# Output projection with two token tiles' products ahead of the last quotient instead of four; first up weights split behind the last values

## The chip, the cores and the metric

The kernel runs on one core of a Trainium2 chip. The metric is the device time of one execution in microseconds (us). The core has five engines that run side by side, each with its own instruction queue in fixed order: TensorE (PE in the profile; PEld is its weight load), VectorE (DVE), ScalarE (ACT), GpSimd (POOL) and SyncE (SP), which here issues nearly all DMAs. Engines wait for each other by semaphores. Matmul results land in PSUM, in banks of 128 x 512 float32; all else on the chip lies in SBUF. The 128 partitions are the first number of every tile shape.

## The reference, cut to what matters

One decoder block on 1024 tokens of width 1024. Eight attention heads of width 64 with a forgetting bias and a gated part of width 512 run side by side; their outputs, concatenated, go through the output projection and are added to the input. A gated MLP with a causal convolution follows, then a last norm.

```python
    mix = jnp.concatenate([att, sg], axis=-1)
    h = h + mix @ w_out[layer]
    h = h + conv_ffn(rmsnorm(h, norm_ffn_g[layer]), w_up[layer], conv_w[layer],
                     conv_b[layer], w_down[layer])
return rmsnorm(h, norm_final_g)
```

In `forgetting_attention` each row of weights is a softmax: exponentials divided by their sum. The kernel multiplies the exponentials with the values first and divides by the row sums at the end. This division is what the title calls the quotient.

## The kernel before, in words

All matmuls work in a reduced-precision form of float32 that the kernel makes up for by splitting: a tensor x becomes a high part (a cast) and a low part (x minus the high part), and a product is three matmuls: high x high, high x low, low x high. `split_w` (L160 to L166) does this for weights: the cast on ACT, the subtraction on DVE. For the up and down projections the kernel uses a seven-product scheme (Strassen, Winograd's form) with block names A11, A12, A21, A22 for weights and S1 to S4 for their sums; the sums of raw weights are made on POOL (`upw_b`, L1271 to L1283). For the first two of the 22 column blocks of the up projection these sums are written in place, over the raw weights that A11 and A12 were split from: so POOL can begin as soon as the split of A11 has read them.

**The end of attention.** Heads are handled in pairs; `attF[p]` (tag H) holds the undivided result of pair p in its first half and the broadcast reciprocals of the row sums in its second. The last values are matmuls at L1054; ACT copies one half of a result (L1062), DVE adds the other (L1063). The reciprocals travel through DRAM: ACT's queue writes them (L943), SP reads them back as a broadcast (L944). Then `pair_half` forms the quotient (L957), casts its high part into `attT[p]` (L958) and subtracts for the low part (L959), in two halves of 512 tokens: 512 to 1023 first, then 0 to 511. For pairs 0 to 2 this is POOL's work, hidden under later heads; for pair 3, the last, it is done by DVE and ACT, and nothing of attention is left to hide it.

**The output projection.** The product of the gated half has been made earlier and stored as `hpd`. What is left is `att @ w_out[:512]`: eight token tiles of 128 (index tt), two column halves (hf), four pairs (k), three matmuls each, 24 matmuls per tile (`wmm`, L1303 to L1305). The tile of `attT` is the stationary operand, the weights move. For tiles 0, 4, 1 and 5 the products of pairs 0 to 2 are made first, into eight PSUM banks, since they need no pair 3: 72 matmuls. Then, tile by tile (0, 4, 1, 5, 2, 3, 6, 7), the rest is accumulated, `hload` brings in `hpd` (L1309), `hadd` adds (DVE, L1313), `norm2` forms the norm (ACT L1320, L1321, DVE L1322, L1323) and stores `h2d` (SP, L1324), and `flip` transposes the normed tile on PE in eight transpositions (L1341) and splits it into the operands of the up projection (L1327 to L1358). Tiles tt and tt + 4 are combined there, which is why their order is interleaved.

**What sets the order.** A scheduler places instructions by its own estimates of time within the data dependencies and the extra orderings that the code adds with `after(later, earlier)`; from then on each engine keeps that order. `seq` chains PE's instructions in the order in which they are written: it was used up to the last values, not in `wmm` and `flip`. `behind` orders an instruction behind one kept in `gates`. The splits of the first up weights (raw tiles loaded at L1252, `upw_a`) went into tag `wha` of a pool that only exists once attention's buffers are released. Tag `x1` held the heads' query and key tiles, two buffers of 128 x 2 x 1024.

Of the kernel before, what the change touches and what calls it, by code (L numbers as in the profile page):

```python
# [14 lines left out]
P = 128  # L15
# [54 lines left out]
def block_kernel(ctx: ExitStack, tc: tile.TileContext, xT, xtok, wuv, wuh, wv0, wva, wvk, wvl, wqk, cpk, bfv,  # L70
# [5 lines left out]
    sml = ctx.enter_context(tc.tile_pool(name="sml", bufs=4))  # L76
    early = tc.alloc_tile_pool(name="early", bufs=1)
# [13 lines left out]
    BUFS = {"x1": 2, "x2": 2, "t3": 1, "t2": 1, "t01": 1, "V": 4, "H": 4, "wy": 2, "gg": 2,  # L91
# [4 lines left out]
    def sb(tag, shape, dt=F32):  # L96
        return (raws if tag == "raw" else late if tag in LATE else early).tile(shape, dt, tag=tag, bufs=BUFS[tag], name=nm(tag))

# [58 lines left out]
    def split_w(src, hl, hi_eng="act", lo_eng="dve"):  # L157
        h, l = hl
        if hi_eng == "act":
            act.copy(h, src)  # L160
# [5 lines left out]
        return eng.tensor_tensor(out=l, in0=src, in1=f32(h), op=ALU.subtract)  # L166

    gates = {}
# [9 lines left out]
    def xset(tags):  # L178
        return [sb(t, [P, 2, 2, 512], F32R) for t in tags]
# [5 lines left out]
    def xs(n, hl, k):  # L185
        return XS[n][k // 2][:, hl, k % 2, :]

    def x2(n, hl, j):
        return XS[n][j][:, hl, :, :]
# [433 lines left out]
    def emit(t, dst, i, parts, src=None):  # L623
        for o in parts:
# [5 lines left out]
            for j in range(2):  # L630
                floors["sp"] = sp.dma_start(out=dst[2 * i + j].rearrange("s d t -> d s t")[:, :, o], in_=t[j * 64:(j + 1) * 64, :, o])

# [80 lines left out]
    floors = {}  # L713
# [16 lines left out]
    xy = sb("x1", [P, 2, 1024])  # L730
    xl = sb("pt", [P, 1024])
    sp.dma_start(out=xl, in_=vx[0])
    after(tc, sp.dma_start(out=xy, in_=vx[1:3].rearrange("a p c -> p a c")), floors["ld"])
    for i, o in ((0, ALU.subtract), (1, ALU.add)):
        after(tc, dve.tensor_tensor(out=xy[:, i], in0=xy[:, i], in1=xl, op=o), newest[0])
    vw["S1"] = pairs(l21)

# [130 lines left out]
    def head_loads(h):  # L868
        ab = sb("x1", [P, 2, 1024], F32R)
        abs_[h] = ab  # L870
        hh = h % 2
        sp.dma_start(out=f32(ab[:, 0, :]), in_=qd[h].rearrange("s d t -> (s d) t"))
        for s in range(2):
            sp.dma_start(out=f32(ab[s * 64:s * 64 + 64, 1, :]), in_=kd[h, 0])
# [10 lines left out]
    va_, vb_, vc_ = xy[:, 0], xy[:, 1], xl  # L885
# [61 lines left out]
    def pair_half(p, o):  # L947
# [8 lines left out]
        else:  # L956
            dve.tensor_tensor(out=f[:, 0, o], in0=f[:, 0, o], in1=f[:, 1, o], op=ALU.mult)  # L957
# [18 lines left out]
    def logits_mm(h, j, ps):  # L976
        A, B, A2, B2 = abs_[h][:, 0, :], abs_[h][:, 1, :], a2s[:, h % 2, :], b2s[:, h % 2, :]
# [237 lines left out]

    for o in (slice(512, 1024), slice(0, 512)):
        pair_half(3, o)


    after(tc, act.activation(pad[:, 0:1], eps, AF.Sqrt), last_copy)  # L1220
# [20 lines left out]
    def ut_(pool_, tag, shape, dt, bufs):  # L1241
        return pool_.tile(shape, dt, tag=tag, bufs=bufs, name=nm(tag))

    xt = {n: xtp.tile([P, 4, 512], F32, tag="xt" + n, name="xt" + n) for n in ("B11", "B21", "B22")}

    AHEAD = 2
    split_of = {}

    def upw_a(i):

        wr = sb("raw", [P, 2, 512])
        d = sp.dma_start(out=wr, in_=wup[i, :, 2:4, :])  # L1252
        if i < AHEAD:
            after(tc, d, loads[7])
        out = {"ra": wr}

        def split(names):
            for n in names:
                t = ut_(upl, "wha", [P, 2, 512], F32R, 4)
                split_of[n] = split_w(wr[:, ("A11", "A12").index(n), :], (t[:, 0], t[:, 1]))  # L1260
                behind(split_of[n], "sums" if i < AHEAD else "hg")
                out[n] = t
            return out

        return out, split
# [33 lines left out]
    def wmm(tt, hf, ps, ks_):  # L1299
        ts_ = slice(tt * P, (tt + 1) * P)  # L1300
        for k in ks_:
            w = wo[k][hf]
            pe.matmul(ps, attT[k][:, 0, ts_], w[:, 0, :], start=(k == 0), stop=False)  # L1303
            pe.matmul(ps, attT[k][:, 0, ts_], w[:, 1, :], start=False, stop=False)
            pe.matmul(ps, attT[k][:, 1, ts_], w[:, 0, :], start=False, stop=(k == 3))  # L1305
# [27 lines left out]
    def flip(tt):  # L1333
# [3 lines left out]
        for kh in range(2):  # L1337
            ps = sbank()
            for j in range(4):
                k = 4 * kh + j  # L1340
                pe.transpose(ps[:, j * P:(j + 1) * P], xn[tt][:, k * P:(k + 1) * P], ident)  # L1341
# [18 lines left out]

    WA = [upw_a(i) for i in range(AHEAD)]
    W = [WA[0][1](("A11", "A12"))]
# [5 lines left out]
    W.append(WA[1][1](("A11", "A12")))  # L1368
    WB = [upw_b(0, W[0], True), upw_b(1, W[1], True)]
    prev = None  # L1370
    for tt in (0, 4, 1, 5, 2, 3, 6, 7):
        hload(tt)
        for hf in range(2):
            if tt in first:
                wmm(tt, hf, banks8[tt, hf], (3,))
                hadd(tt, hf, banks8[tt, hf])
            else:
                ps = bank()
                wmm(tt, hf, ps, range(4))
                hadd(tt, hf, ps)  # L1380
        norm2(tt)
        if prev is not None:
            flip(prev)
        prev = tt
# [236 lines left out]
    RING = {"xr": (upl, "sg", 4), "xh": (upl, "wha", 4), "wh": (upr, "whb", 6)}  # L1621
# [223 lines left out]
```

## Time and profile before

| | us |
|---|---|
| time, median of 3 runs (lowest to highest) | 1046.32 (1046.3 to 1047.15) |
| the profiled execution's own time | 1046.16 |
| its span, first to last instruction | 1044.4 |
| PE busy in the span | 1036.8 |
| DVE / ACT / POOL busy | 893.3 / 562.8 / 222.6 |
| start of the output projection on PE | 357.45 |
| first matmul there that reads the last quotient | 373.87 |

Times in the trace are counted from the first instruction. A timeline row gives start, length, engine, line, operation, output <- inputs, partitions x elements, how many, and in brackets how long the engine stood idle before and what ended that wait. Rows with a count merge instructions of one kind that follow each other; their length runs from the first's start to the last's end. An instruction on DVE or ACT can start some 0.1 us before the one ahead of it has ended, so lengths add up to a little more than the time that passes.

### The profile page before, as it was taken

What the parts mean: (1) busy time and instruction counts of PE and PEld (TensorE: products, weight loads), DVE (VectorE), ACT (ScalarE), POOL (GpSimd) and SP (SyncE); (2) the same over time, 40 slices, a digit from 0 to 9 for tenths busy, and PEclk for the clock granted to TensorE, in tenths of its full rate; (3) what the DMA queues carried; (4) which work ended last, traced back from release to release, by engine and by line L of the source; (5) the groups of instructions that cost most, each with busy time, mean ns of one, the idle gap of its engine ahead of it and who ended that gap; (6) DMA issues with size and microseconds to landing.
All of it is one profiled execution on the core that took longest, in us unless ns stands there. A gap on an engine that the chain in (4) does not pass through costs nothing.

```text
span 1044.4 us, 14270 instructions
## 1 busy us (share of the span) xinstructions
PE 1036.8 (99%) x4998; PEld 870.0 (83%) x4998; DVE 893.3 (86%) x1302; ACT 562.8 (54%) x1003; POOL 222.6 (21%) x167
## 2 busy tenths in 40 slices
PE   9999999999999999999999999999999999999997
PEld 7988888988888888788888888888888888888886
DVE  6899887988888779998999998898997866997774
ACT  6777632457776747644444444443544544454654
POOL 0000232500322540353334323323331000000000
PEclk9999999999999999999999999999999999999999
DMA  9622558885745533231354431332422998333432
GB/s 331 235 85 95 153 156 250 232 259 170 203 135 167 201 134 130 81 120 62 121 168 146 142 121 67 127 111 73 129 81 83 325 337 292 112 92 101 144 118 101
DMA packets 67452, 161.66 MB, mean 155 GB/s; under 512 B 8095, under 2 KB 9239, under 8 KB 67381
## 3 DMA queue, kind: packets, MB, share of 16 engines
q1 hardware_dynamic: 67108, 160.72, 47.9%
q8 instruction: 39, 0.64, 0.3%
q14 instruction: 33, 0.26, 0.1%
q10 hardware_dynamic: 272, 0.04, 0.0%
HBM read 115.68 MB, written 45.05 MB: 154 GB/s over the span
## 4 chain that ended last, share of the span: by engine, by line
PE 98%; DVE 1%; ACT 0%; issue 0%; ACTq 0%; DVEq 0%
PE k L1656 20%; PE qc L1396 12%; PE qa L1396 11%; PE qd L1396 11%; PE qb L1396 5%; PE pb L270 5%; PE ps L270 5%; PE pb L1054 3%; PE pb L1038 3%; PE qc L509 2%; PE qd L509 2%; PE qa L509 2%; PE pl L984 2%; PE ps L853 2%; PE pl L985 2%; PE pf L1078 1%
## 5 line engine op out<-in xcount | busy, mean ns | idle before, releaser
L1656 PE MATMUL k<-whb,wha 128*128 128x512 f32 (+1 forms) x936 | 209.9, 387 | 0.0
L1656 PEld LDWEIGHTS k<-whb,wha 128*128 128x128 f32 x936 | 174.1, 188 | 35.8 <-DVE wha L166 0.2
L1396 PE MATMUL qc<-xT,whb 128*128 128x512 f32 x540 | 129.8, 389 | 0.1
L1396 PE MATMUL qa<-xB,wha 128*128 128x512 f32 x528 | 127.5, 390 | 0.0
L1396 PEld LDWEIGHTS qc<-xT,whb 128*128 128x128 f32 x540 | 101.3, 188 | 21.5 <-ACT whb L160 0.5
L1396 PEld LDWEIGHTS qa<-xB,wha 128*128 128x128 f32 x528 | 98.8, 188 | 20.9 <-DVE wha L166 0.4
L160 ACT CAST wha<-sg 128x512 fp32r<-128x512 f32 x77 | 47.8, 622 | 96.6 <-PE k L1656 84.9
L160 ACT CAST whb<-sg 128x512 fp32r<-128x512 f32 x82 | 50.5, 618 | 87.9 <-PE qc L1396 67.6
L166 DVE TENSOR_TENSOR wha<-sg,wha 128x512 fp32r<-128x512 f32 x77 | 52.8, 688 | 39.0 <-ACT wha L160 38.9
L1396 PE MATMUL qd<-xB,whb 128*128 128x512 f32 x264 | 63.7, 389 | 0.0
L1396 PE MATMUL qd<-xT,whb 128*128 128x512 f32 x264 | 63.7, 390 | 0.0
L1396 PE MATMUL qb<-xT,whb 128*128 128x512 f32 x252 | 61.0, 390 | 0.0
L166 DVE TENSOR_TENSOR whb<-sg,whb 128x512 fp32r<-128x512 f32 x82 | 57.0, 697 | 4.4 <-ACT whb L160 4.3
L1280 POOL TENSOR_TENSOR sg<-raw 128x512 f32<-128x512 f32 x20 | 31.0, 1550 | 139.4 <-DVE whb L166 76.2
L1039 ACT CAST pt<-pb 128x512 fp32r<-128x512 f32 x72 | 40.1, 583 | 36.0 <-PE pb L1038 23.7
L1396 PEld LDWEIGHTS qd<-xT,whb 128*128 128x128 f32 x264 | 49.5, 188 | 10.5 <-DVE u L1503 0.3
L1396 PEld LDWEIGHTS qd<-xB,whb 128*128 128x128 f32 x264 | 49.6, 188 | 10.3
L1396 PEld LDWEIGHTS qb<-xT,whb 128*128 128x128 f32 x252 | 47.2, 188 | 10.0 <-DVE whb L166 0.3
L1040 DVE TENSOR_TENSOR pt<-pb,pt 128x512 fp32r<-128x512 f32 x72 | 47.3, 686 | 9.6 <-ACT pt L1039 8.9
L1054 PE MATMUL pb<-pt,V 128*128 128x512 f32 (+3 forms) x192 | 49.4, 362 | 0.4 <-DVE pt L1040 0.3
L1283 POOL TENSOR_TENSOR sg<-sg,raw 128x512 f32<-128x512 f32 x20 | 33.3, 1664 | 63.5 <-DVE whb L166 63.5
L1281 POOL TENSOR_TENSOR sg<-sg,raw 128x512 f32<-128x512 f32 x20 | 35.1, 1756 | 47.2 <-issue 44.6
(431 smaller groups left out, 2247.6 us busy)
## 6 DMA issues: line engine op xcount, KB each, us to landing
raw<-wup SPq DMA_DIRECT2D x44, 512.0 KB
sg<-hx SPq DMA_DIRECT2D x77, 256.0 KB
hx<-hs SPq DMA_DIRECT2D x44, 256.0 KB
hx<-ca SPq DMA_DIRECT2D x35, 256.0 KB
xT<-wdn SPq DMA_DIRECT2D x28, 256.0 KB
x<-kd SPq DMA_DIRECT2D x24, 256.0 KB
A<-xtok SPq DMA_DIRECT2D x8, 512.0 KB
raw<-wqk SPq DMA_DIRECT2D x8, 512.0 KB
```

Source lines behind the costliest of these rows:

```text
L160: act.copy(h, src)
L166: return eng.tensor_tensor(out=l, in0=src, in1=f32(h), op=ALU.subtract)
L270: pe.matmul(banks[m], xs(n, xi, k)[:, ms], w[:, wi, :], start=(first and k == 0 and c == 0 and (own or m % 2 == 0)), stop=(k == 3 and c == ...
L509: pe.matmul(ps, w[:, wi, ks], xs(n, xi, k), start=(first and c == 0), stop=(c == 11), skip_group_check=True)
L1038: seq(pe.transpose(ptr[:, o:o + P], places[g[0], j // 2][j % 2][:, k * P:(k + 1) * P], ident))
L1039: casts.append(act.copy(pt[:, 0, :], ptr))
L1040: los.append(dve.tensor_tensor(out=pt[:, 1, :], in0=ptr, in1=f32(pt[:, 0, :]), op=ALU.subtract))
L1054: seq(pe.matmul(po[half][:, o:o + w], lhs, pt[:, s, c:c + w], start=(new and s == 0), stop=(s == 1 and (half, k) in ((1, 6), (0, 3))), ski ...
L1281: pool.tensor_tensor(out=s[1], in0=s[0], in1=a11, op=ALU.add)
L1283: pool.tensor_tensor(out=s[3], in0=s[1], in1=a12, op=ALU.add)
L1396: pe.matmul(ps, w[:, wi, ks], xb[:, xi, k, :], start=(first and n == 0), stop=(n == 11), skip_group_check=True)
L1656: pe.matmul((banks[bk + m] if ps is None else ps)[:, o], xh[:, xi, ms], wh[:, wi, o], start=((first and p_ == 0 or new) and n == 0), stop= ...
```

## The change

Five edits, of which the first two are named in the title.

1. `AHEAD`, `upw_a` and its splits move ahead of `pair_half(3, ...)`. The four splits (A11 and A12 of the first two column blocks) are ordered behind the last copy of the values on ACT (`last_copy`), and the first multiplication of the last quotient is ordered behind the last of the four on DVE (`gates["own"]`). The table load for the square root follows the last cast.
2. Only tiles 0 and 4 are started ahead of the quotient: 36 matmuls in four banks.
3. `wmm` and `flip` (but for tile 7's) are chained with `seq`, so PE runs them as written; a table `FLIP` says behind which tile and half each tile's transpositions stand.
4. To have a home before attention's buffers are released, the splits go into tag `x1`, which becomes four buffers of half the size in a pool of its own (`base`); query and key tiles and the value sums become two tiles each. Later splits of A11 and A12 and the down projection's `xh` use the same buffers.
5. The load of the value sums is two DMAs instead of one, with orderings among stores and additions.

```diff
+            m = dve.tensor_tensor(out=f[:, 0, o], in0=f[:, 0, o], in1=f[:, 1, o], op=ALU.mult)
+            if gates:
+                after(tc, m, gates.pop("own"))
...
+            for n in names:
+                t = ut_(base, "x1", [P, 2, 512], F32R, 4)
+                split_of[n] = split_w(wr[:, ("A11", "A12").index(n), :], (t[:, 0], t[:, 1]))
+                if i < AHEAD:
+                    after(tc, cast[0], last_copy)
+                else:
+                    behind(split_of[n], "hg")
...
+    WA = [upw_a(i) for i in range(AHEAD)]
+    W = [a[1](("A11", "A12")) for a in WA]
+    gates["own"] = split_of["A12"]
     for o in (slice(512, 1024), slice(0, 512)):
         pair_half(3, o)
-    after(tc, act.activation(pad[:, 0:1], eps, AF.Sqrt), last_copy)
+    after(tc, act.activation(pad[:, 0:1], eps, AF.Sqrt), cast[0])
...
-    first = (0, 4, 1, 5)
-    banks8 = {(tt, hf): (bank() if hf == 0 else sbank()) for tt in first for hf in range(2)}
-    for hf in range(2):
-        for tt in first:
-            wmm(tt, hf, banks8[tt, hf], (0, 1, 2))
+    early_ = ((0, 0), (4, 0), (0, 1), (4, 1))
+    banks8 = {(tt, hf): (bank() if hf == 0 else sbank()) for tt, hf in early_}
+    for tt, hf in early_:
+        wmm(tt, hf, banks8[tt, hf], (0, 1, 2))
...
+    FLIP = {(1, 1): 0, (5, 0): 4, (2, 0): 1, (3, 0): 5, (6, 0): 2, (7, 0): 3, (7, 1): 6}
     for tt in (0, 4, 1, 5, 2, 3, 6, 7):
         hload(tt)
         for hf in range(2):
-            if tt in first:
-                wmm(tt, hf, banks8[tt, hf], (3,))
-                hadd(tt, hf, banks8[tt, hf])
-            else:
-                ps = bank()
-                wmm(tt, hf, ps, range(4))
-                hadd(tt, hf, ps)
-        norm2(tt)
-        if prev is not None:
-            flip(prev)
-        prev = tt
+            ps = banks8[tt, hf] if (tt, hf) in early_ else bank()
+            wmm(tt, hf, ps, (3,) if (tt, hf) in early_ else range(4))
+            hadd(tt, hf, ps)
+            if hf:
+                norm2(tt)
+            if (tt, hf) in FLIP:
+                flip(FLIP[tt, hf])
```

How the built programs differ, first on DVE at the end of attention. Before (H is `attF[3]`, G is `attT[3]`, wha the split weights, raw the raw ones, pt the loaded `hpd`, pb and ps PSUM banks):

```order
L1063 TENSOR_TENSOR H_3593<-pb_3828,H_3593 64x512
L957 TENSOR_TENSOR H_3593<-H_3593 128x512 x2
L959 TENSOR_TENSOR G_3839<-H_3593,G_3839 128x512 x2
L166 TENSOR_TENSOR wha_3872<-raw_3868,wha_3872 128x512
L166 TENSOR_TENSOR wha_3875<-raw_3868,wha_3875 128x512
L166 TENSOR_TENSOR wha_3958<-raw_3870,wha_3958 128x512
L166 TENSOR_TENSOR wha_3961<-raw_3870,wha_3961 128x512
L1313 TENSOR_TENSOR pt_3978<-pb_3878,pt_3978 128x512
```

With the change (line numbers are those of the changed kernel; x is tag `x1`):

```order
L1080 TENSOR_TENSOR H_3608<-pb_3843,H_3608 64x512
L167 TENSOR_TENSOR x_655_3858<-raw_3854,x_655_3858 128x512
L167 TENSOR_TENSOR x_656_3861<-raw_3854,x_656_3861 128x512
L167 TENSOR_TENSOR x_657_3864<-raw_3856,x_657_3864 128x512
L167 TENSOR_TENSOR x_658_3867<-raw_3856,x_658_3867 128x512
L972 TENSOR_TENSOR H_3608<-H_3608 128x512 x2
L976 TENSOR_TENSOR G_3870<-H_3608,G_3870 128x512 x2
L1335 TENSOR_TENSOR pt_3953<-pb_3899,pt_3953 128x512
```

The four splits have moved from behind the quotient's four instructions to ahead of them; ACT's four casts have moved in the same way, ahead of the table load. POOL's eight sums in place, before:

```order
L1275 TENSOR_TENSOR raw_3868<-raw_3964,raw_3868 128x512
L1276 TENSOR_TENSOR sg_3966<-raw_3868,raw_3964 128x512
L1277 TENSOR_TENSOR raw_3964<-raw_3964 128x512
L1283 TENSOR_TENSOR raw_3868<-sg_3966,raw_3868 128x512
L1275 TENSOR_TENSOR raw_3870<-raw_3971,raw_3870 128x512
L1276 TENSOR_TENSOR sg_3973<-raw_3870,raw_3971 128x512
L1277 TENSOR_TENSOR raw_3971<-raw_3971 128x512
L1283 TENSOR_TENSOR raw_3870<-sg_3973,raw_3870 128x512
```

and with the change:

```order
L1298 TENSOR_TENSOR raw_3854<-raw_3939,raw_3854 128x512
L1300 TENSOR_TENSOR raw_3939<-raw_3939 128x512
L1298 TENSOR_TENSOR raw_3856<-raw_3946,raw_3856 128x512
L1300 TENSOR_TENSOR raw_3946<-raw_3946 128x512
L1299 TENSOR_TENSOR sg_3941<-raw_3854,raw_3939 128x512
L1299 TENSOR_TENSOR sg_3948<-raw_3856,raw_3946 128x512
L1306 TENSOR_TENSOR raw_3854<-sg_3941,raw_3854 128x512
L1306 TENSOR_TENSOR raw_3856<-sg_3948,raw_3856 128x512
```

The same eight sums stand in another order; the first still overwrites the block from which the first of the four splits reads. On PE, the end of the products made ahead, with the change (G_3870 is the last quotient, G_3697 the one before it):

```order
L1327 MATMUL ps_3902<-whl_3732,A_2863 128x512 x3
L1327 MATMUL ps_3902<-whl_3740,A_3297 128x512 x3
L1327 MATMUL ps_3902<-G_3747,G_3697 128x512 x3
L1327 MATMUL pb_3899<-G_3754,G_3870 128x512 x3
L1327 MATMUL ps_3901<-G_3754,G_3870 128x512 x3
L1327 MATMUL pb_3900<-G_3754,G_3870 128x512 x3
L1327 MATMUL ps_3902<-G_3754,G_3870 128x512 x3
L1327 MATMUL pb_3987<-whl_3731,A_2863 128x512 x3
```

The first product with the last quotient is the 37th matmul of the projection, for token tile 0, where it was the 73rd.

More of the change, by code (lines that the diff above doesn't have):

```diff
@@ L96, in sb @@
     def sb(tag, shape, dt=F32):
-        return (raws if tag == "raw" else late if tag in LATE else early).tile(shape, dt, tag=tag, bufs=BUFS[tag], name=nm(tag))
+        return (base if tag == "x1" else raws if tag == "raw" else late if tag in LATE else early).tile(shape, dt, tag=tag, bufs=BUFS[tag], name=nm(tag))
     def bank():
@@ L159, in split_w @@
         if hi_eng == "act":
-            act.copy(h, src)
+            cast[:] = [act.copy(h, src)]
         elif hi_eng == "pool":
@@ L166, in split_w @@
         return eng.tensor_tensor(out=l, in0=src, in1=f32(h), op=ALU.subtract)
-    gates = {}
+    gates, cast = {}, []
     def behind(inst, key):
@@ L1239, in block_kernel @@
         xb_tile(upl, n)
-    def ut_(pool_, tag, shape, dt, bufs):
-        return pool_.tile(shape, dt, tag=tag, bufs=bufs, name=nm(tag))
     xt = {n: xtp.tile([P, 4, 512], F32, tag="xt" + n, name="xt" + n) for n in ("B11", "B21", "B22")}
[L1246 to L1265, printed above, removed]
     def upw_b(i, out, inplace=False):
```

73 lines of the change are left out of this document (49 added, 24 removed).

## The prediction

> **What bounds the kernel now.** I read the page's busy shares first, then the stage of the output projection on TensorE (PE) in the timeline, then the three engines that feed it. The page:
>
> ```profile
> PE 1036.8 (99%) x4998; PEld 870.0 (83%) x4998; DVE 893.3 (86%) x1302; ACT 562.8 (54%) x1003; POOL 222.6 (21%) x167
> PE 98%; DVE 1%; ACT 0%; issue 0%; ACTq 0%; DVEq 0%
> ```
>
> PE is busy for 1036.8 of 1044.4 us and carries 98% of the chain that ended last. So a wait that is put in front of PE lengthens the program by its whole length, and no rearrangement can gain more than the 7.6 us in which PE stands idle, most of it elsewhere. PE in the changed stage (timeline: start, length, what):
>
> ```profile
> 357.45 0.45 PE L1303 MATMUL pb<-whl,A 128*128 128x512 f32 x1
> 365.71 0.39 PE L1303 MATMUL ps<-whl,A 128*128 128x512 f32 x1
> 366.16 0.39 PE L1305 MATMUL ps<-whl,A 128*128 128x512 f32 x1
> 373.87 0.39 PE L1303 MATMUL pb<-G,G 128*128 128x512 f32 x1
> ```
>
> The projection starts at 357.45. 36 matmuls later it is 365.71, 72 matmuls later 373.87; only there does PE first read the last quotient (G,G). It never waits in between. The engines that make that quotient, VectorE (DVE) first:
>
> ```profile
> 358.26 0.68 DVE L1063 TENSOR_TENSOR H<-pb,H 64x512 f32<-64x512 f32 x1 [0.60 <-ACT H L1062]
> 362.36 1.29 DVE L957 TENSOR_TENSOR H<-H 128x512 f32<-128x512 f32 x2 [3.41 <-DMA H<-rsd]
> 363.74 1.29 DVE L959 TENSOR_TENSOR G<-H,G 128x512 fp32r<-128x512 f32 x2
> 364.95 1.28 DVE L166 TENSOR_TENSOR wha<-raw,wha 128x512 fp32r<-128x512 f32 x2
> 366.15 3.47 DVE L166 TENSOR_TENSOR wha<-raw,wha 128x512 fp32r<-128x512 f32 x2
> 374.75 0.69 DVE L1313 TENSOR_TENSOR pt<-pb,pt 128x512 f32<-128x512 f32 x1 [5.12 <-PE pb L1305]
> ```
>
> DVE idles 3.41 us for the broadcast of the reciprocals, multiplies twice, subtracts twice, and has the quotient whole at 363.74 + 1.29 = 365.03, 8.84 us before PE wants it. Then come the four low parts of the first up weights. The first two take 1.28 together, the last two 3.47: the same instruction, nearly three times as long. What changes between them is on GpSimd (POOL):
>
> ```profile
> 365.71 1.67 POOL L1275 TENSOR_TENSOR raw<-raw,raw 128x512 f32<-128x512 f32 x1 [12.72 <-DMA pt<-hpd]
> 367.46 1.62 POOL L1276 TENSOR_TENSOR sg<-raw,raw 128x512 f32<-128x512 f32 x1
> 369.04 1.74 POOL L1277 TENSOR_TENSOR raw<-raw 128x512 f32<-128x512 f32 x1
> 370.74 1.29 POOL L1283 TENSOR_TENSOR raw<-sg,raw 128x512 f32<-128x512 f32 x1
> 367.85 1.77 DVE L166 TENSOR_TENSOR wha<-raw,wha 128x512 fp32r<-128x512 f32 x1
> ```
>
> POOL begins its sums in place of the raw weights at 365.71, 0.76 us after the first DVE split began, that is, as soon as that split has read what the sum overwrites. (The label names a DMA as releaser; the first split's end, about 365.63, fits.) From there the two engines take turns: POOL's first sum ends at 367.38, the third split ends 0.55 later; POOL's second ends at 369.08, the fourth split ends at 369.62. A DVE instruction then stands 1.70 us after its predecessor (366.15 to 367.85) instead of 0.60. It is not any DVE work that suffers:
>
> ```profile
> L1040 DVE TENSOR_TENSOR pt<-pb,pt x72: 672/690/693, 223.7 to 356.3; 128x512 fp32r<-128x512 f32 x72
> L1111 POOL TENSOR_TENSOR whl<-raw,whl x4: 1292/1295/1299, 337.2 to 344.5; 128x512 fp32r<-128x512 f32 x4
> ```
>
> (minimum, median, maximum in ns.) With one operand in PSUM (pb) DVE never exceeds 693 ns, and POOL's sums beside it never 1299. The turns are taken only when both of DVE's inputs lie in SBUF.
>
> **The change part by part.** *Fewer products ahead.* PE now has 36 matmuls ahead of the quotient instead of 72. Their pace and that of a transposition, from the chain of waits:
>
> ```profile
> 445.11 2.72 PE qd L1396 x12
> 394.40 0.87 PE ps L1341 x8
> ```
>
> 2.72/12 = 0.227 us each. The first matmul that reads the quotient stands at 365.71, the third, which reads its low part, at 366.16: the cover falls from 8.84 to 366.16 - 365.03 = 1.13 us. If nothing else moved, no wait.
>
> *Splits first.* The four casts of the first up weights go on ScalarE (ACT) right behind the last copy of the values, their subtractions on DVE ahead of the multiplications.
>
> ```profile
> 357.65 0.58 ACT L1062 COPY H<-pb 64x512 f32<-64x512 f32 x1 [0.82 <-PE pb L1054]
> 364.21 2.18 ACT L160 CAST wha<-raw 128x512 fp32r<-128x512 f32 x4
> 363.08 1.22 ACT L958 CAST G<-H 128x512 fp32r<-128x512 f32 x2 [3.33 <-DVE H L957]
> 358.25 1.28 ACT L1220 ACT_TABLE_LOAD   x1
> ```
>
> ACT: last copy ends at 358.23, four casts of 0.52 step until 360.4, table load until 361.7, still ahead of the 363.08 at which it was wanted: free. DVE: the first cast ends at 358.25 + 0.62 = 358.87, so the first split stands at 358.9, the second at 359.5, the third would at 360.1. Undisturbed, the fourth ends at 361.4, inside the 3.41 us idle gap, and the quotient would still be whole at 365.03.
>
> But the first split releases POOL, now at 358.9 + 0.76 = 359.7, and POOL has eight sums of at least 1.29 us, over ten us of work without a pause. Behind the second split stand six DVE instructions with both inputs in SBUF: splits three and four, two multiplications, two subtractions. At one per 1.70 us: 360.1 + 6 x 1.70 = 370.3, with the last one's own end 370.37. The broadcast (362.3) is in by the time the multiplications come up at 363.5, so it no longer sets anything. PE holds the low part's matmul from 366.16 to 370.37, 4.2 us. The quotient is the stationary operand there, so a weight load comes on top:
>
> ```profile
> L1396 PEld LDWEIGHTS qc<-xT,whb 128*128 128x128 f32 x540 | 101.3, 188 | 21.5 <-ACT whb L160 0.5
> ```
>
> 188 ns make 4.4 us. Bounds: nothing (undisturbed), and 4.6 with a semaphore's delay at both hand-overs. I take 4.4, since the rows with the same instructions on both sides are the disturbed ones. Queued behind PE's wait is all that follows on PE; behind DVE's turns are the additions of the projection, which have a PSUM operand and aren't slowed.
>
> The Trainium skill ("SBUF — State Buffer", Who interferes with whom) says that a DVE instruction with two SBUF inputs and a GpSimd instruction that reads SBUF shut each other out whole, and that the order of issue decides who is blocked. The trace agrees on the first (1.77 against 0.68 us). On the second the page leaves open who comes next when both wait; if DVE, queued up, kept its turn throughout, its wait would be nothing and the sum would be that of the first rival. The rows show strict turns, and the sum goes by them.
>
> *Transpositions in written order.* Before, they are scattered into matmuls:
>
> ```profile
> 383.55 0.61 PE ps L1341 x4
> 385.79 1.06 PE ps L1341 x8
> 419.90 5.44 PE qc L1396 x24
> ```
>
> 357.45 to 419.90 holds 240 matmuls and 64 transpositions: 240 x 0.2267 + 8 x 0.87 = 61.4 of 62.45 us, so 1.1 us is lost there. Two rows name some of it: 0.61 for four (half of 0.87 is 0.44) and 1.06 for eight, 0.36 together. I take 0.6 as gained, bounds 0 and 1.1. Does the fixed order make PE wait for a norm? Tile 0's transpositions stand 30 matmuls, 6.8 us, behind its last product; before, the second addition ended about 376.1 and the transpositions came at 380.38, 4.3 us; with 0.7 for the addition that leaves some 1.8 us. No wait; if that cover were gone, DVE's lag on each pair would show one for one. The next loads of the hidden state stand behind one store each on SP's queue and have a tile of slack.
>
> *POOL's other order, x1 in four buffers, the split load of the value sums, weight splits in the new buffers:* the order of instructions ahead of 357 is the same but for one DMA cut in two. Nothing.
>
> Sum: 1046.16 + 4.4 - 0.6 = 1049.96 against the profiled execution's time (span 1044.4 and 1.76 around it); that run lies 0.16 under the median, so 1050.1.
>
> **Rivals.** *Not slower: the turns don't cost.* Place: DVE between the second split and the last subtraction. If DVE keeps its turn, or POOL comes later, the quotient is whole by 366.1 and only the 0.6 is left: 1045.7. It decides at the third slowed instruction of the six: with the splits alone slowed the multiplications start at 363.5 instead of 362.36, 1.14 later, which the cover of 1.13 still takes; each further one costs 1.1. Four slowed of six with all of the 1.1 gained: 4.4 - 2 x 1.1 - 1.1 = +1.1, 1047.4. For it: POOL's timing rests on one inferred release. Against: the rows of the turns are these very instructions. 0.14.
>
> *PE's clock falls in the wait.* Place: PE behind the wait.
>
> ```profile
> PE ps L126 <- DVE pad L137: 1.3, 1, 1.3
> PEclk9999999999999999999999999999999999999999
> ```
>
> The longest wait of PE in this trace is 1.3 us and the granted clock is at 90% or more in every slice, so it shows nothing for 4 us. If PE ran at half speed afterwards for as long as it stood, 2.2 us are added: 1052.3. Against: two matmuls that need only the cast (ready about 367.6) break the wait into 1.9 and 2.3 us. 0.08. The Trainium skill ("TensorE: Matmul & The Clock Gate", Part 1) gives about 3.4 us idle for the clock to halve; by that figure neither piece is long enough.
>
> *Faster by more than 0.2%:* 2.1 us would need all 1.1 of the stage and as much again from waits that the change doesn't touch. 0.04.
>
> **How the numbers follow.** The turns cost what the rows say: 0.74, 1050.1. With the clock's 0.08 that is 0.82 slower; 0.14 same; 0.04 faster. A difference of 0.2% (2.1 us) is about what a measurement of this kernel can tell from no change. The range runs from four slowed of six, 1047.4, to the clock's case, 1052.3.
>
> **What would show it.** Right: POOL's first sum near 359.7; splits three and four and the quotient's four DVE instructions near 1.7 us each; the last subtraction's end near 370.4; one PE wait of about 4.4 us on it (in two pieces) ahead of the first k = 3 products; transpositions at 0.87 per eight. Wrong: those DVE instructions at 0.68, or PE going from the 36th to the 37th matmul without a gap; or a wait of PE at a transposition.

## The result, and the profile after

| | before | changed |
|---|---|---|
| median of 5 runs, us | 1046.32 (1046.23 to 1047.15) | 1051.93 (1051.4 to 1053.32) |
| ratio, 95% interval | | 1.0054 (1.004 to 1.0068) |
| profiled run: time, span, us | 1046.16, 1044.4 | 1051.93, 1050.2 |
| first matmul of the projection, us | 357.45 | 357.70 |
| first qc matmul of the up stage, us | 419.73 | 425.47 |
| from one to the other ("the stage"), us | 62.28 | 67.77 |

The changed kernel is 5.6 us slower. The stage, read from the starts of two matmuls in the timeline, is 5.49 us longer; the work ahead of it took 0.25 us more, all of it gathered in the first 28 us, where both kernels run their instructions in the same order, and the work behind it 0.06 us more. So the loss lies in the 68 us of the projection. (The chain's row for qc, 419.90 in the prediction, begins 0.16 us later, where the matmul before ends.) I use the stage for each experiment below, since the time outside it varies by more than a microsecond from run to run. Its value is that of the one profiled run of each kernel.

The changed kernel's page, busy time by engine and the chain that ended last:

```profile
PE 1038.4 (99%) x4998; PEld 870.9 (83%) x4998; DVE 896.8 (85%) x1302; ACT 564.4 (54%) x1003; POOL 223.5 (21%) x167
...
PE 96%; DVE 2%; ACT 1%; issue 0%; DMA 0%; SPq 0%; DVEq 0%; ACTq 0%
```

DVE and ACT now hold 3% of the chain together, where before it was 1%. PE's busy time grew by 1.6 us with the same 4998 matmuls: some of them became longer. The changed kernel's waits of PE (us in total, times, longest) name the place:

```profile
PE pb L1327 <- ACT G L975: 2.0, 1, 2.0
PE pb L1327 <- DVE G L976: 1.9, 1, 1.9
```

Neither was there before. G is the last quotient: PE waits first for its high part (ACT), then for its low part (DVE). The changed kernel's DVE timeline (start, length, what):

```profile
359.23 4.68 DVE L167 TENSOR_TENSOR x<-raw,x 128x512 fp32r<-128x512 f32 x4
363.84 3.46 DVE L972 TENSOR_TENSOR H<-H 128x512 f32<-128x512 f32 x2
367.22 3.42 DVE L976 TENSOR_TENSOR G<-H,G 128x512 fp32r<-128x512 f32 x2
```

The four splits now come first and take 4.68 us; the pair of multiplications, 1.29 us before, takes 3.46, and the pair of subtractions, 1.29 before, 3.42. The quotient is whole at 367.22 + 3.42 = 370.64. Beside them, the changed kernel's POOL timeline:

```profile
360.00 1.67 POOL L1298 TENSOR_TENSOR raw<-raw,raw 128x512 f32<-128x512 f32 x1 [6.80 <-DVE x L167]
361.75 1.61 POOL L1300 TENSOR_TENSOR raw<-raw 128x512 f32<-128x512 f32 x1
...
366.70 3.38 POOL L1299 TENSOR_TENSOR sg<-raw,raw 128x512 f32<-128x512 f32 x2
370.05 2.96 POOL L1306 TENSOR_TENSOR raw<-sg,raw 128x512 f32<-128x512 f32 x2
```

POOL begins 0.77 us after the first split (now with the split itself named as releaser) and is at work until 373.01. And PE:

```profile
365.26 0.84 PE L1327 MATMUL ps<-G,G 128*128 128x512 f32 x3
368.09 0.70 PE L1327 MATMUL pb<-G,G 128*128 128x512 f32 x2 [1.99 <-ACT G L975]
370.69 0.50 PE L1327 MATMUL pb<-G,G 128*128 128x512 f32 x1 [1.89 <-DVE G L976]
...
371.93 1.48 PE L1327 MATMUL pb<-G,G 128*128 128x512 f32 x3
```

The 36th matmul ends at 366.10, two matmuls that need the high part alone stand in the middle, and the third of the group comes at 370.69. What I had given little chance is in the last row: three matmuls take 1.48 us where the first row has 0.84 for three. The changed kernel in stretches of 1 us (stretch, its length, then PE, weight loads, DVE, ACT and POOL, then the granted clock, the DMA share and GB/s):

```profile
370.00:371.00 1.00, 0.31 (x1) 0.30 (x2) 0.63 (x1) 0.00 (x0) 1.00 (x2) 1.00 0.00 0
371.00:372.00 1.00, 1.00 (x5) 0.77 (x4) 0.69 (x1) 0.00 (x0) 1.00 (x2) 0.72 0.00 0
372.00:373.00 1.00, 1.00 (x4) 0.81 (x3) 0.69 (x1) 0.10 (x1) 1.00 (x1) 0.50 0.00 0
373.00:374.00 1.00, 1.00 (x3) 0.78 (x3) 0.55 (x1) 1.00 (x2) 0.01 (x1) 0.50 0.31 123
374.00:375.00 1.00, 1.00 (x4) 0.76 (x3) 0.41 (x2) 0.34 (x2) 0.00 (x0) 0.57 0.99 401
```

The clock stood at half for (0.28 + 0.50 + 0.50 + 0.43) / 0.5 = 3.4 us, while PE was fully busy again. Matmuls then follow each other every 0.427 us instead of 0.227. In 40 slices of the page this can't be seen: each still shows a 9. The mean granted clock of the span shows it in every run: it is 0.995 to 0.997 in the five runs above and in five more below, and never under 0.998 in the runs of before beside the experiments. Last, the transpositions, in the changed kernel's chain:

```profile
380.32 0.87 PE ps L1363 x8
```

0.87 for eight, whole, where before some were cut up and slower.

### The profile page after: what moved, and what is told of

Same layout as the page of the kernel before. It is cut to its first block, busy times and chain, and to the rows that moved or that the text cites. A ratio compares the mean times of both kernels' runs of the same rounds, so it can differ in the third digit from the quotient of the medians.

```text
span 1050.2 us, 14269 instructions
## 1 busy us (share of the span) xinstructions
PE 1038.4 (99%) x4998; PEld 870.9 (83%) x4998; DVE 896.8 (85%) x1302; ACT 564.4 (54%) x1003; POOL 223.5 (21%) x167
## 4 chain that ended last, share of the span: by engine, by line
PE 96%; DVE 2%; ACT 1%; issue 0%; DMA 0%; SPq 0%; DVEq 0%; ACTq 0%
PE k L1672 20%; PE qc L1412 11%; PE qa L1412 11%; PE qd L1412 11%; PE qb L1412 5%; PE ps L278 5%; PE pb L278 5%; PE pb L1327 3%; PE pb L1071 3%; PE pb L1055 3%; PE qc L517 2%; PE qd L517 2%; PE qa L517 2%; PE pl L1001 2%; PE ps L868 2%; PE pl L1002 2%
## 5 line engine op out<-in xcount | busy, mean ns | idle before, releaser
L1672 PE MATMUL k<-whb,x 128*128 128x512 f32 (+1 forms) x936 | 209.9, 386 | 0.0
L1672 PEld LDWEIGHTS k<-whb,x 128*128 128x128 f32 x936 | 174.1, 188 | 35.8 <-DVE x L167 0.2
L1412 PE MATMUL qa<-xB,x 128*128 128x512 f32 x528 | 127.3, 390 | 0.0
L1412 PEld LDWEIGHTS qa<-xB,x 128*128 128x128 f32 x528 | 98.8, 188 | 20.9 <-DVE x L167 0.4
L161 ACT CAST x<-sg 128x512 fp32r<-128x512 f32 x77 | 47.7, 621 | 97.0 <-PE k L1672 83.7
L167 DVE TENSOR_TENSOR x<-sg,x 128x512 fp32r<-128x512 f32 x77 | 52.8, 687 | 39.2 <-ACT x L161 39.0
```

What stands on the lines that cost most here:

```text
L161: cast[:] = [act.copy(h, src)]
L1412: pe.matmul(ps, w[:, wi, ks], xb[:, xi, k, :], start=(first and n == 0), stop=(n == 11), skip_group_check=True)
L1672: pe.matmul((banks[bk + m] if ps is None else ps)[:, o], xh[:, xi, ms], wh[:, wi, o], start=((first and p_ == 0 or new) and n == 0), stop= ...
```

## The experiments

Theory: the splits released POOL early, DVE and POOL took turns, so the quotient came late (PE idle), and because PE was idle its clock fell; the written order of the transpositions gave a little back. Rivals: the splits ahead cost by themselves (1), two tiles ahead are too few in any case (2), and for the slow matmuls, that they have another cause than idle time. All of these kernels start from the changed kernel, but for two that start from the one before.

| kernel | stage, us | median, us | runs | ratio to before, 95% interval |
|---|---|---|---|---|
| POOL's sums held back | 61.71 | 1045.99 | 11 | 0.999 (0.9981 to 0.9999) |
| splits behind the quotient | 62.33 | 1047.61 | 11 | 1.0009 (1.0001 to 1.0018) |
| half of the splits ahead | 63.14 | 1046.95 | 11 | 1.0007 (0.9999 to 1.0016) |
| 18 filler matmuls | 66.22 | 1050.27 | 5 | 1.0035 (1.0021 to 1.0049) |
| 9 filler matmuls | 66.22 | 1051.18 | 5 | 1.0043 (1.0031 to 1.0056) |
| 4 filler matmuls | 69.04 | 1052.2 | 5 | 1.0055 (1.0042 to 1.0067) |
| wait in one piece | 69.31 | 1054.06 | 5 | 1.0068 (1.0055 to 1.008) |
| changed kernel again | 68.44 | 1052.36 | 5 | 1.0058 (1.0045 to 1.0071) |
| four tiles ahead | 65.47 | 1049.75 | 7 | 1.0031 (1.002 to 1.0043) |
| before, written order alone | 65.96 | 1050.31 | 5 | 1.0034 (1.0021 to 1.0046) |
| before, written order, later | 61.88 | 1046.64 | 11 | 1.0002 (0.9993 to 1.0011) |
| four tiles ahead, later | 61.89 | 1047.15 | 11 | 1.0007 (0.9998 to 1.0015) |

The runs of before beside them had medians of 1046.48, 1046.63 and 1046.24 in the three groups of four in which the kernels were run.

**POOL's sums held back.**

```diff
-            pool.tensor_tensor(out=a11, in0=a21, in1=a11, op=ALU.add)
+            if not hold:
+                hold.append(pool.tensor_copy(s[1][:, 0:1], f32(attT[3][:, 1, 0:1])))
+            after(tc, pool.tensor_tensor(out=a11, in0=a21, in1=a11, op=ALU.add), hold[0])
...
+    hold = []
```

> The changed kernel with one alteration: POOL's eight sums start only when the last quotient is whole (a one-element POOL copy of its low part stands ahead of them). Splits ahead and 36 matmuls ahead stay. Theory (DVE's six instructions take turns with POOL's sums): without POOL each of the six takes about 0.68 us instead of 1.7, the quotient is whole at about 365.3 us, PE (wants it at 366.4) doesn't wait, no slow matmuls, 1045.7 us (before less 0.6 for the transpositions). Rival 1 (the splits by themselves put the quotient late, whatever POOL does): PE still waits 4 us, 1050 to 1052. Rival 2 (two tiles ahead are too few in any case): 1049 to 1052.

DVE of this kernel:

```profile
358.57 2.50 DVE L167 TENSOR_TENSOR x<-raw,x 128x512 fp32r<-128x512 f32 x4
362.34 1.29 DVE L972 TENSOR_TENSOR H<-H 128x512 f32<-128x512 f32 x2 [1.27 <-DMA H<-rsd]
363.72 1.30 DVE L976 TENSOR_TENSOR G<-H,G 128x512 fp32r<-128x512 f32 x2
```

and its POOL, held by the one-element copy until the subtractions have ended:

```profile
365.08 0.19 POOL L1299 COPY sg<-G 128x1 f32<-128x1 f32 x1 [12.51 <-DVE G L976]
```

The same DVE instructions in the same order as in the changed kernel, with only POOL out of the way: 2.50 instead of 4.68, 1.29 instead of 3.46, 1.30 instead of 3.42. The quotient is whole at 365.02 and PE doesn't wait; no matmul is slow. Both rivals fall: splits ahead and two tiles ahead cost nothing without POOL. The time is 0.1% under before, with an interval that just leaves out no change, and 0.6% under the changed kernel: of the versions run, this one is the fastest. The turns are not gone, they have moved: POOL's sums now run beside the norm of the first token tile, and its DVE instruction takes 2.13 us, where the changed kernel needs 1.28 for it (at 375.53, with POOL already done).

```profile
369.27 2.13 DVE L1347 SCALAR_TENSOR_TENSOR xn<-pt,ss,g2b 128x1024 f32<-128x1024 f32 x1
```

There PE has other products to run, and no wait follows.

**Splits behind the quotient** (and the multiplications no longer held behind them).

```diff
-            m = dve.tensor_tensor(out=f[:, 0, o], in0=f[:, 0, o], in1=f[:, 1, o], op=ALU.mult)
-            if gates:
-                after(tc, m, gates.pop("own"))
+            dve.tensor_tensor(out=f[:, 0, o], in0=f[:, 0, o], in1=f[:, 1, o], op=ALU.mult)
...
+                    behind(split_of[n], "quot")
...
+    for o in (slice(512, 1024), slice(0, 512)):
+        gates["quot"] = pair_half(3, o)
     W = [a[1](("A11", "A12")) for a in WA]
-    gates["own"] = split_of["A12"]
-    for o in (slice(512, 1024), slice(0, 512)):
-        pair_half(3, o)
```

> The changed kernel with the four splits moved back behind the last quotient's subtractions, as they stood before; 36 matmuls ahead and the written order of the transpositions stay. Theory: POOL is released only after the quotient, which is whole at about 365.3 us, 1.1 us ahead of PE's need: no wait, 1045.7 us. Rival 1 (splits by themselves): also 1045.7. Rival 2 (two tiles ahead are too few): 1049 to 1052, with a PE wait on the quotient of 3 us or more.

No wait on the quotient, as the theory has it, and so rival 2 falls again; the time of 1047.61 is a miss. Of the 1.9 us above the forecast, 0.62 lie in the stage: the additions of the projection now stand behind the splits and start 11.9 us after its first matmul (370.85), where they start 9.1 us after it with the sums held back (366.15), so the first norm is late and PE waits 0.26 us at a transposition, which is part of the 0.62. More lies far ahead of the change: in the profiled run PE waited once in a stage near 219 us,

```profile
PE pl L999 <- DVE mn L55: 1.2, 1, 1.2
```

because DVE had waited for a load there:

```profile
218.67 0.69 DVE L55 TENSOR_TENSOR raw<-pf,raw 128x512 f32<-128x512 f32 x1 [1.52 <-DMA raw<-xtok]
```

That this wait came oftener in this kernel's runs than in others' isn't shown; only the one run was profiled.

**Half of the splits ahead.**

```diff
+                    behind(split_of[n], "quot")
...
-    W = [a[1](("A11", "A12")) for a in WA]
+    W = [WA[0][1](("A11", "A12"))]
     gates["own"] = split_of["A12"]
     for o in (slice(512, 1024), slice(0, 512)):
-        pair_half(3, o)
+        gates["quot"] = pair_half(3, o)
+    W.append(WA[1][1](("A11", "A12")))
```

> The changed kernel with only the first column block's two splits ahead of the multiplications, the other two behind the subtractions. POOL, in its order, gets only four of its eight sums released (two run in DVE's idle gap, two beside the multiplications). Theory of turns: about three of the quotient's four DVE instructions are slowed instead of six of six, quotient whole at about 367.4 us, PE waits 1.0 to 1.4 us, clock not halved, 1046.9 us (1046.4 to 1047.4). Rival 1 (the splits themselves, half of them): half of the loss of 5.6, 1048.8. Rival 2 (two tiles ahead are too few): 1049 to 1052.

DVE of this kernel, PE's wait, and POOL around its pause, each from its own view:

```profile
361.89 2.96 DVE L972 TENSOR_TENSOR H<-H 128x512 f32<-128x512 f32 x2 [1.79 <-DMA H<-rsd]
364.77 2.38 DVE L976 TENSOR_TENSOR G<-H,G 128x512 fp32r<-128x512 f32 x2
```

```profile
PE pb L1329 <- DVE G L976: 0.9, 1, 0.9
```

```profile
364.38 1.62 POOL L1308 TENSOR_TENSOR raw<-sg,raw 128x512 f32<-128x512 f32 x1
367.89 1.63 POOL L1300 TENSOR_TENSOR raw<-raw,raw 128x512 f32<-128x512 f32 x1 [1.89 <-DVE x L167]
```

POOL has four sums and then pauses at 366.00. The multiplications beside it are slow (2.96), of the two subtractions only the first (2.38). The quotient is whole at 367.15, 0.25 earlier than expected, PE waits 0.9 us, and 1046.95 is what the theory of turns gives (1046.9). The cost follows the number of DVE instructions that meet POOL, not the number of splits ahead.

**Filler matmuls of 18, 9 and 4.** The fillers add work whose result nobody reads (shown for 18; the others differ in the number alone).

```diff
+    spare = sbank()
+    for _ in range(18):
+        seq(pe.matmul(spare, attT[0][:, 0, 0:P], wo[0][0][:, 0, :], start=True, stop=True))
```

> The changed kernel with 18 matmuls more, on operands that are long ready, written into a spare bank that nobody reads, between the 36th and the 37th matmul (about 4.1 us, the length of the wait). The quotient stays as late as in the changed kernel. Theory (the 8 matmuls at 0.427 us behind the wait come from PE having stood idle): PE has no idle stretch over 0.6 us there, no slow matmul, 1.6 us less than the changed kernel, 1050.3. Rival (the slow matmuls come from something else, such as the other engines' work at that time): slow matmuls stay, 1051.9 or more.

> The changed kernel with 9 matmuls more on operands long ready, into a spare bank that nobody reads, between the 36th and the 37th: about 2.0 us, so that only the second idle stretch of 1.9 us (for the quotient's low part) is left. Theory 1 for the slow clock (it falls where PE was busy for too small a share of about 3.4 us; one stretch of 1.9 is under 60% idle): no slow matmul, 1050.3 us as with 18. Theory 2 (a stretch of about 1.9 us is enough by itself): eight matmuls at 0.427 us behind it, 1051.9.

> The changed kernel with 4 matmuls more into a spare bank that nobody reads: PE's first idle stretch falls from 2.0 to about 1.1 us, the second (1.9) stays. If the clock is halved where PE was busy for under about two fifths of 3.4 us: 3.0 us idle in 3.5 is near that bound and falls or not by where the 3.4 us begin, so stage 66.2 us in some runs and 67.8 in others, 1050.3 to 1051.9. If two stretches of nearly 2 us each are needed: 1050.3 in all.

18 of them: 1050.27, as expected from the idle time. With 9, PE still idles for 1.92 us in one piece (PE of that kernel):

```profile
369.14 0.70 PE L1327 MATMUL pb<-G,G 128*128 128x512 f32 x2
371.77 0.50 PE L1327 MATMUL pb<-G,G 128*128 128x512 f32 x1 [1.92 <-DVE G L976]
372.10 0.85 PE L1327 MATMUL ps<-G,G 128*128 128x512 f32 x3
```

No slow matmul follows (0.85 for three), and the stage is 66.22 us, as with 18; its median is higher by 0.9, in part since the work ahead of the stage took longer (the projection starts at 358.72 in its profile, at 358.05 with 18). One of its four other runs took 1052.44 us at a mean clock of 0.997, the value of runs in which the clock fell: one piece seems to be enough in some runs and not in others, but that run has no profile. With 4, PE idles for 1.11 and 1.90 us, and the clock fell in the profiled run, for twice as long as in the changed kernel; 14 matmuls were slow, the stage took 69.04, and four of the five runs took 1051.79 us or more at a mean clock of 0.996 or 0.997, where a clock that stays whole would give 1050.3; the fifth took 1050.50 at 0.998. So it fell in some runs and not in others, as the expectation had it, though the price in the profiled run was higher. That two pieces of nearly 2 us each are needed is refuted.

**The wait in one piece.**

```diff
-            for n, (a, b) in enumerate(((0, 0), (0, 1), (1, 0))):
+            for n, (a, b) in enumerate(((1, 0), (0, 0), (0, 1)) if k == 3 else ((0, 0), (0, 1), (1, 0))):
```

> The changed kernel with the last quotient's low part first in each group of three, so that PE's wait is one stretch of about 4.2 us instead of two with two matmuls between. Those two matmuls now follow the wait: +0.45 us. Theory 1 (too small a busy share of about 3.4 us halves the clock): slow matmuls in each run, 1052.4 us with a spread of some 1 us. Rival (only a window of 3.4 us without any matmul halves the clock, and the two pieces fell to it by something else): the fall would come in about one run of four, most runs 1050.8.

PE of this kernel:

```profile
371.64 1.62 PE L1327 MATMUL pb<-G,G 128*128 128x512 f32 x3 [4.68 <-DVE G L976]
373.06 1.48 PE L1327 MATMUL ps<-G,G 128*128 128x512 f32 x3
```

All five runs took 1052.79 us or more, at a mean clock of 0.995 or 0.996: the rival's one run in four doesn't fit. The price was 1.7 us over what I expected: in the stretches of this run the clock is at half for 6.8 us, not 3.4, so 12 matmuls are slow.

**The changed kernel again**, without an edit.

> The changed kernel itself once more, for a second profile. Theory: quotient whole at 370.4 to 370.9 us, PE idle for 3.9 us in two pieces, half the clock for 3.41 us behind them, stage 67.8 us, 1051.9 us. If the fall of the clock was a chance of that one run: stage 66.1 us, 1050.3.

PE of that run:

```profile
367.59 0.74 PE L1327 MATMUL pb<-G,G 128*128 128x512 f32 x2 [2.00 <-ACT G L975]
370.19 0.80 PE L1327 MATMUL pb<-G,G 128*128 128x512 f32 x1 [1.86 <-DVE G L976]
```

and its stretches of 1 us around the fall and at its end:

```profile
367.00:368.00 1.00, 0.41 (x2) 0.30 (x2) 1.00 (x1) 0.45 (x1) 1.00 (x2) 1.00 0.00 0
368.00:369.00 1.00, 0.33 (x2) 0.00 (x0) 1.00 (x2) 0.00 (x0) 1.00 (x1) 0.56 0.00 0
...
374.00:375.00 1.00, 1.00 (x3) 0.77 (x3) 0.41 (x2) 0.48 (x3) 0.00 (x0) 0.53 1.05 422
```

The same two idle pieces, and the clock falls again, so it was no chance of one run. But here it falls right behind the first piece and is at half from 368.1 to 374.9, 6.8 us ((0.44 + 5 x 0.50 + 0.47) / 0.5, the five stretches between standing at 0.50); part of that lies in idle time, so 10 matmuls are slow and the stage takes 68.44 instead of 67.77.

**Four tiles ahead**, and **before with the written order alone** (the second is the kernel before with the order of products and transpositions chained as in the change).

```diff
-    early_ = ((0, 0), (4, 0), (0, 1), (4, 1))
+    early_ = [(tt, hf) for hf in range(2) for tt in (0, 4, 1, 5)]
```

> The changed kernel with four token tiles' products ahead again (72 matmuls in eight banks); the splits stay ahead of the quotient. Theory: the turns stay, the quotient is again whole at about 370.5 us, but PE wants it only at about 374: no wait, no slow matmul; the stage from the projection's first matmul to the first qc product takes 61.7 us, as with POOL's sums held back, 1045.9 us. Rival (the late quotient costs elsewhere, the additions behind DVE's turns for example): 1048 or more with the cover back.

> The kernel before with only the written order of products and transpositions; 72 matmuls ahead and splits behind the quotient, as before. Theory (the change's one gain is this order): transpositions at 0.87 us per eight, stage 61.7 instead of 62.28 us, 1045.8 us against 1046.4 for before. Rival (the 0.57 us came from the splits standing ahead): stage stays at 62.3, 1046.4.

Both are misses, by 4 us. With four tiles ahead PE needn't wait for the quotient, as expected, but (PE of that kernel):

```profile
377.54 0.84 PE L1327 MATMUL ps<-G,G 128*128 128x512 f32 x3
380.36 1.09 PE L1363 MATMUL ps<-ident,xn 128*128 128x128 f32 x8 [1.98 <-DVE xn L1345]
...
383.89 0.66 PE L1363 MATMUL ps<-ident,xn 128*128 128x128 f32 x4 [1.30 <-ACT xtB L1371]
```

When all but the last three of twelve matmuls of a product are done ahead, the place "behind the second product of tile 1" comes 12 matmuls (2.7 us) after tile 0's last product instead of 30, and tile 0's norm isn't ready. The kernel before with that order has the same wait of 1.98 us on the norm with its quotient early, so the late quotient isn't the reason. I had moved one part of the change without seeing that its table of places holds only for two tiles ahead.

**The same two with later places.**

```diff
-    FLIP = {(1, 1): 0, (5, 0): 4, (2, 0): 1, (3, 0): 5, (6, 0): 2, (7, 0): 3, (7, 1): 6}
+    FLIP = {(2, 0): 0, (2, 1): 4, (3, 0): 1, (6, 0): 5, (6, 1): 2, (7, 0): 3, (7, 1): 6}
```

> The kernel before (72 matmuls ahead, splits behind the quotient) with a written order in which each tile's transpositions come one to two products later than in the changed kernel (tile 0's behind the first product of tile 2 instead of the second of tile 1). Theory (the written order gains what the scattered transpositions lose; the 3.7 us lost in the kernel with the changed kernel's positions came from norms not yet ready there): no wait at a transposition, stage 61.7 us against 62.28, 1045.8 us. Rival (a fixed order costs by itself): stage over 63 us, 1047 or more.

> The changed kernel with 72 matmuls ahead and the same later transpositions; splits ahead, POOL's turns and the late quotient (370.5 us) stay. Theory (the late quotient costs only as far as PE has nothing else to do): no wait at the quotient or at a transposition, stage 61.7 us, 1045.8 us, 5 to 6 under the changed kernel. Rival (the late quotient costs elsewhere): stage over 63 us, 1047 or more.

The stages are 61.88 and 61.89 us, without a wait on quotient or norm. So a late quotient (whole at 371.2 with four tiles ahead) costs nothing where PE has 72 matmuls to do, and a written order takes 0.4 us out of the stage of before by itself, by one profile of each. The times, 1046.64 and 1047.15, are above the 1045.8 of the expectation, the second even where the rival put it, but not by a longer stage: in the profiles the gain is given back behind it (PE of before with the later order):

```profile
PE qd L1397 <- DVE u L1504: 0.8, 1, 0.8
```

PE waits there once for an addition of DVE, which works almost without a pause (24.9 of the 25 us from 407 to 432); four tiles ahead has 0.7 there. The addition ends at 428.98, in before at 428.77, 0.06 us ahead of its matmul: a PE that comes earlier only waits longer. With POOL's sums held back, where the transpositions stand earlier, it ends at 427.63 and PE doesn't wait. That their later places are the reason is likely, not shown.

## Why the prediction was right, and where its sum fell short

*The direction and the mechanism* were right: slower, by turns of DVE and POOL that make the quotient late. Holding POOL's sums back alone takes the whole loss away.

*POOL's release*: 359.7 forecast, 360.00 measured, in a run in which the stage began 0.25 later. *The turns*: the third split starts about 359.23 + 2 x 0.60 = 360.43, the last subtraction ends at 370.64, six instructions in 10.2 us, the 1.70 each of the sum. *The quotient*: 370.37 forecast, 370.64 measured, the difference being that 0.25 again. The Trainium skill ("SBUF — State Buffer", Who interferes with whom) leaves open who comes next when both wait; here the two engines took turns one for one, and the rival built on the other reading, 1045.7, is out. The additions, with one operand in PSUM, took 0.69 us beside POOL (at 371.22 and 372.17), not slowed, as was said.

*PE's wait*: 4.4 us forecast. The kernels with 18 and 9 fillers, in which the quotient is as late but no matmul is slow, have a stage 66.22 - 61.71 = 4.51 us longer than the one with POOL held back. The pieces were 2.0 and 1.9, near the 1.9 and 2.3 forecast.

*The transpositions*: 0.6 gained, bounds 0 and 1.1; the stage with POOL held back is 62.28 - 61.71 = 0.57 shorter than before. That no norm would be waited for held in the changed kernel: tile 0's norm ended 2.0 us ahead of its transpositions with POOL held back (371.40 and 373.43) and 3.35 in the changed kernel (376.81 and 380.16), where 1.8 was worked out. The runs with four tiles ahead show what stands behind that cover.

*What failed is the step on PE's clock.* I set it at a chance of 0.08, since "two matmuls that need only the cast (ready about 367.6) break the wait", and left it out of the sum. The clock fell in both profiled runs of the changed kernel: 67.77 - 66.22 = 1.55 us in the first, 68.44 - 66.22 = 2.22 in the second. The stage's growth is then -0.57 + 4.51 + 1.55 = 5.49; that these add up says nothing by itself, since each is a difference of two measured stages. What bears the account out is that the forecast had 0.6 and 4.4 for the first two, and that 8 matmuls at 0.427 instead of 0.227 us make 1.6, near the third. The forecast of 1050.1 is what the kernel with 18 fillers takes (1050.27). The changed kernel's 1051.93 is the clock rival's case, put at 1052.3. That its price of 2.2 is met by the second profile is luck: it was worked out from a half rate that lasts as long as PE stood, and the half rate lasted 3.4 us in one profile and 6.8 in the other, part of that in idle time.

The break by two matmuls didn't protect, and the traces show why. In each profile the changes of the granted clock lie a whole multiple of 3.413 us apart: in the changed kernel they stand at 371.45, 374.86 (one) and, behind the last matmul, at 1047.29 (197 more). On that grid the stretches with idle pieces are these: the changed kernel (two rows), the same again, before with the written order alone, four tiles ahead (two rows) and 9 fillers, each from its own view. In the last two kernels, where the clock didn't fall near, the grid is counted back from the fall at the program's end (1044.67 and 1047.25, 194 and 198 such lengths behind 382.48 and 371.41). The columns are those of the stretches of 1 us above: behind the stretch and its length stands PE's busy time.

```profile
364.62:368.03 3.41, 1.48 (x7) 0.90 (x5) 3.41 (x3) 1.24 (x2) 3.33 (x3) 1.00 0.17 70
368.03:371.45 3.42, 1.47 (x5) 0.97 (x6) 2.83 (x3) 0.00 (x0) 3.42 (x3) 1.00 0.00 0
364.70:368.12 3.42, 1.42 (x6) 0.69 (x5) 3.42 (x3) 1.24 (x2) 3.42 (x3) 1.00 0.07 26
378.47:381.88 3.41, 1.43 (x11) 1.22 (x11) 3.38 (x6) 1.59 (x5) 0.00 (x0) 1.00 0.94 356
379.07:382.48 3.41, 2.12 (x15) 1.81 (x15) 3.26 (x5) 1.63 (x3) 0.00 (x0) 1.00 0.96 322
382.48:385.90 3.42, 2.12 (x12) 1.75 (x12) 2.70 (x5) 2.53 (x7) 0.00 (x0) 1.00 0.69 237
368.00:371.41 3.41, 1.84 (x8) 0.92 (x6) 3.41 (x3) 0.62 (x1) 3.41 (x3) 1.00 0.03 11
```

The clock fell at the end of the second, third and fourth, in which PE was busy for 1.47, 1.42 and 1.43 us (and behind 1.17 us with 4 fillers, 0.04 with the wait in one piece). It stayed whole behind the others, with 1.48, 2.12, 2.12 and 1.84. These rows fit a clock that goes by PE's busy time in one such stretch, and not one that goes by the length of an idle piece: 1.98 us made it fall in one kernel and not in the other. My estimate from them is a bound near 1.5 of 3.4 us busy; 1.47 and 1.48 are closer to each other than the modelled ends of matmuls can tell apart.

The Trainium skill ("TensorE: Matmul & The Clock Gate", Part 1) asks for about one idle window of 3.4 us, and windows that run freely. The runs agree on the length and on the free running: the grid lies differently from run to run, so that the fall came behind the second idle piece in one profile of the changed kernel and behind the first in the other. They don't agree that PE must be idle for a whole window: in the second profile it had idled for 2.00 us when the clock fell.

## What to carry to other kernels

Work that is moved ahead of a wait brings along what it releases: here it was not the splits on DVE that cost, but the long queue of GpSimd sums that became free with the first of them, and that made every DVE instruction with two SBUF inputs wait its turn. When an edit leaves TensorE idle for about 2 us within 3.4, in one piece or several, expect slow matmuls behind the wait as well (1.5 to 2.8 us in the kernels here with a late quotient) and add them to it. A written order of instructions is good for the cover that it was written for; change how much runs ahead, and its places have to be read again.

## What was not expected of the hardware

- The granted clock fell with idle time far under 3.4 us in one piece: with 2.0 + 1.9 us and two matmuls between (in one profile behind both, in the other behind the first alone), with 1.1 + 1.9, and behind 1.98 us in the kernel before with the written order (at 381.88). It fell in the one wait of 4.7 us too. In the profiled runs it did not fall after a single 1.92, after 0.9, nor after 1.98 and 1.30 with four tiles ahead. The same 1.98 us made it fall where they lay within one stretch of the 3.41 us grid, and not where the grid cut them into 0.69 and 1.29 (four tiles ahead, at 379.07). The bound near 1.5 us busy rests on one profile of each kernel.
- The half rate lasted 3.4 us (the changed kernel's first profile, the kernel before with the written order) or 6.8 us (its second, the wait in one piece, 4 fillers), nothing between. In each of the three longer cases PE was still idle for 0.7 us or more after the fall: the first 3.41 us at half rate held 1.55, 2.10 and 2.65 us of busy time and did not end it, while 2.88 us (before with the written order) and 3.41 (the changed kernel) did.
- With 4 fillers, less idle time than in the changed kernel (3.0 against 3.9 us) gave more slow matmuls (14 against 8 and 10) in the profiled run: where the fall lands matters as much as how long the wait is.
- The work ahead of the stage took between 357.04 and 358.95 us in the profiled runs, though its instructions hardly differ; in three of them DVE waited for a load of the input near 218 us (1.52, 0.57 and 0.54 us). So two kernels that differ by half a microsecond are told apart by the stage, not by their times.
